# Three in four rows of attention's shift and scale summed by TensorE in four column quarters, on one Trainium2 core

## The chip, the core and the metric

The kernel is one block of a hybrid model (short convolution, sparse attention, adaptive layer norm, gated feed-forward) in float32 on one core of a Trainium2 chip. The metric is the device time of one execution, in microseconds. The engines are TensorE (PE in the profile, with its weight loads as PEld), VectorE (DVE), ScalarE (ACT), GpSimd (POOL) and SyncE (SP), which here only issues loads.

## The reference

```python
def rms_norm(x, g):
    xf = x.astype(jnp.float32)
    y = xf * lax.rsqrt(jnp.mean(xf * xf, axis=-1, keepdims=True) + EPS)
    return (y * g.astype(jnp.float32)).astype(x.dtype)

def modulate(h, shift, scale):
    return h * (1.0 + scale[:, None, :]) + shift[:, None, :]
...
sh_a, sc_a, g_a, sh_f, sc_f, g_f = jnp.split(jax.nn.silu(c) @ ada_w[l] + ada_b[l], 6, axis=-1)
h = modulate(rms_norm(x, norm_mix[l]), sh_a, sc_a)
proj = h @ w_in[l]
...
x = x + g_a[:, None, :] * (jnp.concatenate([y_conv, y_attn], axis=-1) @ w_out[l])
h = modulate(rms_norm(x, norm_ffn[l]), sh_f, sc_f)
x = x + g_f[:, None, :] * ((jax.nn.silu(h @ ffn_w1[l]) * (h @ ffn_w3[l])) @ ffn_w2[l])
```

There are 512 tokens and a model width of 2048; `c` is one vector of 2048, `ada_w` is 2048 x 12288, `w_in` is 2048 x 5656. The change concerns `sh_a` and `sc_a`, that is 2 x 2048 columns of `silu(c) @ ada_w`, 33.5 MB of weights.

## The kernel before, in words

Width 2048 is 16 chunks of 128 (`KC`). The start stage loads the four token tiles of x, gets each token's norm on ScalarE, and turns x into 16 chunks `xnT` (channels on partitions, tokens along the row) by float32 multiplications with a diagonal (L278). Then, two chunks at a time (`STEP`), it needs their shift and scale, modulates them on ScalarE (L293), splits the result into a rounded part and its rest (`ahi` L295, `alo` L296), and multiplies with the columns of w_in for raw keys and values, gate logits, selected keys and the first half of the queries. Every such product is three matmuls of 512 columns in the float32r form (L98 to L100, `mm3`), and the weights are split the same way as they are loaded (`load_split`, L91 to L93).

The shift and scale of two chunks come from `start_steps`: twice (scale, then shift) a sum over 2048 rows of a 256-column piece of ada_w. Partition p holds rows 16p to 16p + 15, so there are 16 rows k to add on each partition (a load of 512 KB brings four), and then a sum over partitions. Of the 16, `SHARE` = 6 are scaled by ScalarE (L183) and added by POOL (L185); the other 10 are multiplied and added by DVE (L187, L189), and L192 joins the two. `ada_cols` turns the sum by TensorE (L206, two 128-column transposes), and DVE adds along the row (L208), adds the bias (L210) and, for the scale, applies the norm's gain (L213).

`weave` (the generator helper) sets the order in which the code is written: after each piece of the projections of two chunks (`start_columns`), so many steps of the sums of the next two. Tile's scheduler then reorders each engine's instructions by its own estimates, so what stands in each engine's queue is not what the loop says. Loads of all kinds go through SP's queue in one order; a load that waits for a buffer holds those behind it. The ring of ada_w has four buffers of 512 KB, that of w_in four. TensorE starts its matmuls in queue order. The eight PSUM banks are four `main` buffers, which hold the raw keys and values over the whole stage, and four `aux` buffers, one of which holds the gate logits.

Of the kernel before, what the change touches and what calls it, by code (L numbers as in the profile page):

```python
# [9 lines left out]
F32 = mybir.dt.float32  # L10
F32R = mybir.dt.float32r
I32 = mybir.dt.int32
AF = mybir.ActivationFunctionType
ALU = mybir.AluOpType
# [3 lines left out]
P = 128  # L18
D = 2048
S = 512  # L20
NT = S // P
KC = D // P
# [47 lines left out]
def block_kernel(ctx: ExitStack, tc: tile.TileContext, a: dict, out: bass.AP):  # L70
    nc = tc.nc
# [4 lines left out]
    def pool(name, bufs=1, stack=ctx, **kw):  # L76
        return stack.enter_context(tc.tile_pool(name=name, bufs=bufs, reuse_waits="tile", **kw))
# [24 lines left out]
    def weave(work, side, n):  # L102

        due = 0.0
        for _ in work:
            due += n
            while due >= 1:
                next(side, None)
                due -= 1
        for _ in side:  # L110
            pass
# [14 lines left out]
    ring = rings(ctx, 4, 3)  # L126
    accp = pool("acc", 2)
# [4 lines left out]
    st0 = ExitStack()  # L132
    sp = pool("start", 1, stack=st0)
    cT = cp.tile([P, KC], F32, name="cT")
# [11 lines left out]
    ident, causal = const[:, 0:P], const[:, P:2 * P]  # L146
# [3 lines left out]
    inv, ones = const[:, o:o + HD // 2], const[:, o + HD // 2:o + HD // 2 + P]  # L150
# [7 lines left out]
    cols = cp.tile([P, nrow], F32, name="cols")  # L158
    bcol = cp.tile([P, NB6], F32, name="bcol")
    gsc = cp.tile([P, 2, KC], F32, name="gsc")  # L160
    shf = cp.tile([P, 2, KC], F32, name="shf")
    gts = cp.tile([P, NT, 3 * NH], F32, name="gts")

    ada_v = ada_w.rearrange("(p k) n -> p k n", k=KC)

    def ada_steps(ring, width, c0, n, bias=False, second=None, share=0):


        acc = accp.tile([P, 512], F32, tag="acc", name="acc")[:, :n]
        acc2 = second.tile([P, 512], F32, tag="acc2", name="acc2", bufs=2)[:, :n] if share else None  # L170
        step = min(width // n, KC)
        yield acc
        if bias:
            nc.gpsimd.memset(acc, 0.0)
            nc.sync.dma_start(acc[0:1, :], a["ada_b"][:, c0:c0 + n])
        for k0 in range(0, KC, step):
            raw = ring.tile([P, width], F32, tag="araw", name="araw")
            rv = raw[:, :step * n].rearrange("p (k n) -> p k n", k=step)
            nc.sync.dma_start(rv, ada_v[:, k0:k0 + step, c0:c0 + n])
            for k in range(k0, k0 + step):  # L180
                w, s = rv[:, k - k0, :], cT[:, k:k + 1]
                if k < share:
                    nc.scalar.activation(w if k else acc2, w, AF.Copy, scale=s)  # L183
                    if k:
                        nc.gpsimd.tensor_add(acc2, acc2, w)  # L185
                elif k == share and not bias:
                    nc.vector.tensor_scalar(acc, w, s, None, op0=ALU.mult)  # L187
                else:
                    nc.vector.scalar_tensor_tensor(acc, w, s, acc, op0=ALU.mult, op1=ALU.add)  # L189
            yield  # L190
        if share:
            nc.vector.tensor_add(acc, acc, acc2)  # L192

    def ada(*args, **kw):
        steps = ada_steps(*args, **kw)
        acc = next(steps)
        for _ in steps:
            pass
        return acc

    def ada_cols(psum_tile, acc, which, m, k0, n):

        ps = psum_tile()
        for c in range(n):
            cs = slice(c * P, (c + 1) * P)
            nc.tensor.transpose(ps[:, cs], acc[:, cs], ident)  # L206
        d = (gsc if m else shf)[:, which, k0:k0 + n]
        nc.vector.reduce_sum(d, ps[:, :n * P].rearrange("p (c q) -> p c q", c=n), axis=AX)  # L208
        b0 = (which * 3 + m) * KC + k0
        nc.vector.tensor_add(d, d, bcol[:, b0:b0 + n])  # L210
        if m:
            g0 = at[("norm_mix", "norm_ffn")[which]] + k0
            nc.vector.scalar_tensor_tensor(d, d, 1.0, cols[:, g0:g0 + n], op0=ALU.add, op1=ALU.mult)  # L213
# [14 lines left out]
    ksv = kp.tile([P, NT, 512], F32, name="ksv")  # L228
    q0 = kp.tile([P, NT, 512], F32, name="q0")
    raw_kv = kp.tile([P, 2, NKV, S], F32, name="raw_kv")  # L230
    aring = pool("araw", 4, stack=st0)
    STEP, AW, SHARE = 2, 1024, 6

    def start_steps(k0):

        if k0 < KC:
            for m in (1, 0):
                steps = ada_steps(aring, AW, m * D + k0 * P, STEP * P, second=sp, share=SHARE)
                acc = next(steps)
                yield from steps  # L240
                ada_cols(aux, acc, 0, m, k0, STEP)

    first = start_steps(0)
    vrow = sp.tile([nrow, P], F32, name="vrow")
    brow = sp.tile([NB6, P], F32, name="brow")
    at, r0 = {}, 0
# [13 lines left out]
    for i in range(NT):  # L260
# [8 lines left out]
        dg = sp.tile([P, P], F32, name=f"dg{i}")  # L269
        nc.vector.tensor_scalar(dg, ident, ss, None, op0=ALU.mult)  # L270
        dgs.append(dg)
    for _ in range(KC * STEP * P // AW):
        next(first)
    xnT = []
    for k in range(KC):
        ps = aux()
# [6 lines left out]
    hT = []  # L283
    ps_kv = [main() for _ in range(4)]
    ps_gl = aux()
    for _ in first:
        pass

    def start_columns(k0):
        n = STEP  # L290
        for k in range(k0, k0 + n):
            h = sp.tile([P, S], F32, tag="h", name="h", bufs=2)
            nc.scalar.activation(h, xnT[k], AF.Identity, scale=gsc[:, 0, k:k + 1], bias=shf[:, 0, k:k + 1])  # L293
            hi, lo = parts()
            nc.scalar.copy(hi, h)  # L295
            nc.vector.tensor_sub(lo, h, hi.bitcast(F32))  # L296
            hT.append((hi, lo))
        w = load_split(ring, rows(w_in, k0, n, CKC, 512), n, 512)
        for c in range(4):
            for kk in range(n):  # L300
                mm3(ps_kv[c], [t[:, kk, c * P:(c + 1) * P] for t in w], hT[k0 + kk], k0 + kk == 0, k0 + kk == KC - 1)
            yield
        w = load_split(ring, rows(w_in, k0, n, CGL, P), n, P)
        for kk in range(n):
            mm3(ps_gl, [t[:, kk, :] for t in w], hT[k0 + kk], k0 + kk == 0, k0 + kk == KC - 1)
        yield

        for c0, dst, ends in ((CKS, ksv, (0, 2, 4, 8, 12, 16)), (CQ, q0, (0, 2, 6, 10, 14, 16))):
            if k0 + n not in ends:
                continue  # L310
            ks = range(ends[ends.index(k0 + n) - 1], k0 + n)
            ws = [load_split(ring, rows(w_in, k, 2, c0, 512), 2, 512) for k in ks[::2]]
            for i in range(NT):
                ps = aux()
                tok = slice(i * P, (i + 1) * P)
                for k in ks:
                    mm3(ps, [h[:, tok] for h in hT[k]], [t[:, k % 2, :] for t in ws[(k - ks[0]) // 2]],
                        k == ks[0], k == ks[-1])
                if k0 == 0:
                    nc.scalar.copy(dst[:, i, :], ps)  # L320
                else:
                    nc.vector.tensor_add(dst[:, i, :], ps, dst[:, i, :])
                yield

    for k0 in range(0, KC, STEP):
        weave(start_columns(k0), start_steps(k0 + STEP), 1.3)
    for m in range(2):
        for g in range(NKV):
            (nc.vector.tensor_copy if g else nc.scalar.copy)(raw_kv[:, m, g, :], ps_kv[m * NKV + g])
# [801 lines left out]
```

## Time and profile before

| | us |
|---|---|
| median of 3 runs | 2312.16 (2307.25 to 2317.63) |
| the profiled execution, its time | 2311.1 |
| its span | 2309.3 |
| TensorE busy in the span | 2234.3 (97%) |
| VectorE | 1681.4 (73%) |
| ScalarE | 960.3 (42%) |
| GpSimd | 132.7 (6%) |

Busy time is an average over stages with different limits, so the whole-span shares say little about the start stage. Matmuls overlap in the records (one of 512 columns lasts about 0.39 us, and the next starts 0.23 us after it), so TensorE's cost is read from the distance between starts or ends, not from busy time. The profile's page names lines of the kernel before; all times of the trace are from the span's start. A few matmul records are missing from the trace.

### The profile page before, as it was taken

The numbers are of one execution on the slowest core, as the hardware profiler recorded it, in microseconds if no ns is written. First come the engines' busy times: TensorE is split into PE (matmuls) and PEld (weight loads), VectorE is DVE, ScalarE is ACT, GpSimd is POOL, SyncE is SP. The second block draws the span as 40 slices with busy tenths as digits, with TensorE's granted clock in tenths as the row PEclk, the third lists the DMA queues.
The fourth block names the chain that finished last, engine by engine and source line by source line (L and its number), as shares of the span: only waits on it lengthen the run. The fifth ranks groups of instructions, "written<-read, shape, count | busy, mean of one in ns | idle before, by whom it ended". The sixth has DMA issues, their size and how long they took to land.

```text
span 2309.3 us, 30022 instructions
## 1 busy us (share of the span) xinstructions
PE 2234.3 (97%) x11225; PEld 1861.8 (81%) x11225; DVE 1681.4 (73%) x2561; ACT 960.3 (42%) x1601; POOL 132.7 (6%) x204
## 2 busy tenths in 40 slices
PE   5889999999999999899999999999999999999999
PEld 4667767778777778788888888888888788888887
DVE  6897738877856783888888888888888655534356
ACT  6544425455444222744444444444444432222221
POOL 2430000000000000000000000000000200000010
PEclk9999999999999999999999999999999999999999
DMA  8884356544533883264334443344442675533243
GB/s 292 262 277 148 98 189 184 165 126 147 147 94 128 301 291 128 87 183 123 119 120 124 123 123 120 119 123 124 123 124 78 216 245 187 182 106 128 92 155 114
DMA packets 374406, 358.60 MB, mean 155 GB/s; under 512 B 14856, under 2 KB 288620, under 8 KB 373236
## 3 DMA queue, kind: packets, MB, share of 16 engines
q1 hardware_dynamic: 365364, 325.22, 44.7%
q0 software_dynamic: 8896, 31.46, 3.9%
q8 instruction: 88, 1.44, 0.2%
q14 instruction: 58, 0.48, 0.1%
HBM read 336.70 MB, written 19.92 MB: 154 GB/s over the span
## 4 chain that ended last, share of the span: by engine, by line
PE 42%; issue 36%; DVE 10%; DMA 9%; ACT 2%; POOL 1%; SPq 0%; DVEq 0%; POOLq 0%; ACTq 0%
PE main L98 8%; PE main L99 8%; PE main L100 8%; DMA araw<-in_ada_w 7%; DVE acc L189 4%; PE aux L98 4%; PE aux L99 4%; PE aux L100 4%; PE aux L646 1%; DVE wlo L93 1%; PE main L834 1%; PE aux L834 1%; PE aux L618 1%; POOL gd L886 1%; DMA raw<-in_w_in 1%
## 5 line engine op out<-in xcount | busy, mean ns | idle before, releaser
L92 ACT CAST whi<-raw 128x1024 fp32r<-128x1024 f32 (+1 forms) x168 | 171.7, 1022 | 486.9 <-PE main L100 265.9
L93 DVE TENSOR_TENSOR wlo<-raw,whi 128x1024 fp32r<-128x1024 f32 (+1 forms) x168 | 200.4, 1193 | 223.2 <-ACT whi L92 221.7
L834 PE MATMUL main<-hC,whi 128*128 128x512 f32 x1408 | 356.2, 395 | 5.5 <-DVE hC L851 3.3
L827 DVE TENSOR_TENSOR wlo<-raw,whi 128x1024 fp32r<-128x1024 f32 x218 | 265.8, 1220 | 107.1 <-ACT whi L822 107.1
L189 DVE SCALAR_TENSOR_TENSOR acc<-araw,cT,acc 128x512 f32<-128x512 f32 (+1 forms) x392 | 270.8, 692 | 90.1 <-DMA araw<-in_ada_w 79.3
L822 ACT CAST whi<-raw 128x1024 fp32r<-128x1024 f32 x218 | 228.1, 1046 | 259.5 <-PE main L834 129.4
L834 PEld LDWEIGHTS main<-hC,whi 128*128 128x128 f32 x1408 | 254.4, 190 | 52.2 <-DVE hC L851 4.4
L834 PE MATMUL aux<-hC,whi 128*128 128x512 f32 x1072 | 269.5, 393 | 0.0
L834 PEld LDWEIGHTS aux<-hC,whi 128*128 128x128 f32 x1072 | 193.6, 190 | 34.8
L836 PEld LDWEIGHTS main<-hC,wlo 128*128 128x128 f32 x1408 | 192.9, 191 | 13.8
L836 PE MATMUL main<-hC,wlo 128*128 128x256 f32 x1408 | 197.0, 283 | 0.0
L98 PE MATMUL main<-alo,whi 128*128 128x512 f32 x448 | 180.9, 404 | 9.9 <-DVE alo L296 9.9
L100 PE MATMUL main<-ahi,whi 128*128 128x512 f32 x448 | 177.2, 396 | 0.0
L99 PE MATMUL main<-ahi,wlo 128*128 128x512 f32 x448 | 177.0, 395 | 0.0
L836 PEld LDWEIGHTS aux<-hC,wlo 128*128 128x128 f32 x1072 | 146.4, 190 | 10.5
L98 PE MATMUL main<-wlo,ahi 128*128 128x512 f32 x384 | 152.3, 397 | 0.5 <-DVE t L773 0.4
L100 PE MATMUL main<-whi,ahi 128*128 128x512 f32 x384 | 150.6, 392 | 0.0
L99 PE MATMUL main<-whi,alo 128*128 128x512 f32 x384 | 150.6, 392 | 0.0
L836 PE MATMUL aux<-hC,wlo 128*128 128x256 f32 x1072 | 149.8, 282 | 0.0
L822 ACT CAST whi<-t 128x1024 fp32r<-128x1024 f32 x84 | 88.2, 1050 | 136.4 <-PE aux L834 70.9
L98 PE MATMUL main<-wlo,ghi 128*128 128x512 f32 x352 | 138.2, 394 | 3.0 <-ACT ghi L1056 2.7
L98 PE MATMUL aux<-wlo,ghi 128*128 128x512 f32 x352 | 137.8, 391 | 0.0
(273 smaller groups left out, 3818.8 us busy)
## 6 DMA issues: line engine op xcount, KB each, us to landing
raw<-in_ffn_w SPq DMA_DIRECT2D x264, 512.0 KB
araw<-in_ada_w SPq DMA_DIRECT2D x136, 512.0 KB
araw<-in_ada_w SPq DMA_DIRECT2D x112, 256.0 KB
raw<-in_w_in SPq DMA_DIRECT2D x128, 192.0 KB
raw<-in_w_in SPq DMA_DIRECT2D x40, 512.0 KB
raw<-in_w_out SPq DMA_DIRECT2D x32, 512.0 KB
gd<-d POOLq DMA_DIRECT2D x44, 256.0 KB, 2.3
graw<-gd POOLq DMA_DIRECT2D x44, 256.0 KB, 4.1
```

Source lines behind the costliest of these rows:

```text
L92: nc.scalar.copy(hi[:, :m], raw[:, :m])
L93: nc.vector.tensor_sub(lo[:, :m], raw[:, :m], hi[:, :m].bitcast(F32))
L98: nc.tensor.matmul(ps, lhs[0], rhs[1], start=first, stop=False)
L99: nc.tensor.matmul(ps, lhs[1], rhs[0], start=False, stop=False)
L100: nc.tensor.matmul(ps, lhs[0], rhs[0], start=False, stop=last)
L189: nc.vector.scalar_tensor_tensor(acc, w, s, acc, op0=ALU.mult, op1=ALU.add)
L618: nc.tensor.matmul(one[b], queries(g, i, h), kT[b][g][:, :L], start=True, stop=True)
L646: nc.tensor.matmul(po[:, b * HD:(b + 1) * HD], s["pT"][b][:, kb * P:(kb + 1) * P], vv[b][:, kb, g * HD:(g + 1) * HD], start=kb == 0, stop= ...
L822: nc.scalar.copy(hi, t)
L827: nc.vector.tensor_sub(lo, t, hi.bitcast(F32))
L834: nc.tensor.matmul(ps, wt[0][:, ks[k]], hC[p][:, k, :], start=first and k == 0, stop=False, skip_group_check=True)
L836: nc.tensor.matmul(ps[:, HS:], wt[1][:, ks[k]], hC[p][:, k, 0:HS], start=False, stop=last and k == HK - 1, skip_group_check=True)
```

## The change

`start_steps` now sums the scale and the shift of two chunks together. A load brings four rows k of one of them (512 KB as before); two loads fill one buffer of the ring, which has three buffers of 1 MB. Of each four rows, DVE takes the first (`SHARE` = 1) with one instruction over all 512 columns. TensorE takes the other three: `crep` holds `silu(c)` repeated over 32 columns, and a multiplication of these 32 weight columns with 128 columns of ada_w writes 32 PSUM partitions; four of them, one in each quarter of the array's columns, cover the scale and shift of both chunks. All rows k add up in one `aux` buffer. Four more such multiplications, with ones, add DVE's sum. ScalarE copies the 128 x 128 result (each quarter's 32 partitions hold the same row), one multiplication with four columns of the identity turns it (L253), and DVE adds the bias and applies the gain. ScalarE's scalings, POOL's adds, the transposes and the reductions of this part go. The first unit's sums now stand behind the turning of x in the code, and `weave` takes 0.6 steps where it took 1.3 (a unit has 5 steps now, where it had 8). `ada`, which serves the other parts of ada_w, keeps its path without the share.

```diff
-    def ada_steps(ring, width, c0, n, bias=False, second=None, share=0):
+    def ada(ring, width, c0, n, bias=False):
...
-                if k < share:
-                    nc.scalar.activation(w if k else acc2, w, AF.Copy, scale=s)
-                    if k:
-                        nc.gpsimd.tensor_add(acc2, acc2, w)
-                elif k == share and not bias:
+                if k == 0 and not bias:
                     nc.vector.tensor_scalar(acc, w, s, None, op0=ALU.mult)
                 else:
                     nc.vector.scalar_tensor_tensor(acc, w, s, acc, op0=ALU.mult, op1=ALU.add)
...
-    aring = pool("araw", 4, stack=st0)
-    STEP, AW, SHARE = 2, 1024, 6
+    aring = pool("araw", 3, stack=st0)
+    STEP, SHARE = 2, 1
+    AK, AN = 4, STEP * P
+    crep = sp.tile([P, KC, 32], F32, name="crep")
+    nc.vector.tensor_copy(crep, cT[:, :, None].to_broadcast([P, KC, 32]))
...
-        if k0 < KC:
-            for m in (1, 0):
-                steps = ada_steps(aring, AW, m * D + k0 * P, STEP * P, second=sp, share=SHARE)
-                acc = next(steps)
-                yield from steps
-                ada_cols(aux, acc, 0, m, k0, STEP)
...
+        ps = aux()
+        acc = accp.tile([P, 512], F32, tag="acc", name="acc")
+        begun = [False] * 4
+
+        def quarter(lhs, src, last):
+            for j in range(4):
+                nc.tensor.matmul(ps[32 * j:32 * j + 32, :P], lhs, src[:, j * P:(j + 1) * P], start=not begun[j], stop=last,
+                                 skip_group_check=True)
+                begun[j] = True
+
+        for k in range(0, KC, AK):
+            raw = aring.tile([P, AK, 2 * AN], F32, tag="araw", name="araw")
+            for m in range(2):
+                c0 = m * D + k0 * P
+                nc.sync.dma_start(raw[:, :, m * AN:(m + 1) * AN], ada_v[:, k:k + AK, c0:c0 + AN])
+            for kk in range(AK):
+                w, s = raw[:, kk, :], cT[:, k + kk:k + kk + 1]
+                if kk >= SHARE:
+                    quarter(crep[:, k + kk, :], w, False)
+                elif k + kk == 0:
+                    nc.vector.tensor_scalar(acc, w, s, None, op0=ALU.mult)
+                else:
+                    nc.vector.scalar_tensor_tensor(acc, w, s, acc, op0=ALU.mult, op1=ALU.add)
+            yield
+        quarter(ones[:, 0:32], acc, True)
+        asb = sp.tile([P, P], F32, tag="asb", name="asb", bufs=2)
+        nc.scalar.copy(asb, ps[:, :P])
+        nc.tensor.matmul(ps[:, AN:AN + 4], asb, ident[:, 0:P:32], start=True, stop=True, skip_group_check=True)
+        yield
+        for m, d in ((1, gsc), (0, shf)):
+            d = d[:, 0, k0:k0 + STEP]
+            nc.vector.tensor_add(d, ps[:, AN + m * STEP:AN + (m + 1) * STEP], bcol[:, m * KC + k0:m * KC + k0 + STEP])
+            if m:
+                g0 = at["norm_mix"] + k0
+                nc.vector.scalar_tensor_tensor(d, d, 1.0, cols[:, g0:g0 + STEP], op0=ALU.add, op1=ALU.mult)
...
-        weave(start_columns(k0), start_steps(k0 + STEP), 1.3)
+        weave(start_columns(k0), start_steps(k0 + STEP), 0.6)
```

Two places show how the instructions move. On TensorE, in the start stage before, between the projections of the first two chunks (`main` and `aux` are the PSUM buffers, the numbers tell buffers apart, L206 are the transposes of a sum):

```order
L100 MATMUL main_312<-ahi_366,whi_371 128x512
L206 MATMUL aux_432<-const_87,acc_382 128x128 x2
L98 MATMUL aux_313<-alo_361,whi_450 128x512
L99 MATMUL aux_313<-ahi_360,wlo_451 128x512
L100 MATMUL aux_313<-ahi_360,whi_450 128x512
```

Two transposes there stand for each 16 rows of a scale or shift.

On TensorE after the change, at the end of the projections of the third and fourth chunk (L232 are the quarters, `acc` is DVE's sum, `asb` the copied result of a unit, L253 the turn):

```order
L100 MATMUL aux_717<-whi_656,ahi_575 128x512
L232 MATMUL aux_597<-acc_598,const_87 32x128 x4
L232 MATMUL aux_765<-araw_767,crep_108 32x128 x12
L232 MATMUL aux_765<-araw_795,crep_108 32x128
L253 MATMUL aux_597<-const_87,asb_729 128x4
L232 MATMUL aux_765<-araw_795,crep_108 32x128 x11
L98 MATMUL aux_835<-wlo_825,ahi_569 128x512
L99 MATMUL aux_835<-whi_824,alo_570 128x512
L100 MATMUL aux_835<-whi_824,ahi_569 128x512
```

A unit's last four quarters and its turn now have quarters of the next unit between and behind them. Over the whole stage TensorE's queue has 416 quarters; 64 stand ahead of the first projection matmul, and the other 352 in 33 runs of 1 to 33, each ended by a matmul of another kind.

On SP, from the first load of ada_w, before:

```order
L179 DMA araw<-in_ada_w 128x4x256 x8
L91 DMA raw<-in_w_in 128x2x512
L179 DMA araw<-in_ada_w 128x4x256 x5
L91 DMA raw<-in_w_in 128x2x128
L179 DMA araw<-in_ada_w 128x4x256
```

and after:

```order
L240 DMA araw<-in_ada_w 128x4x256 x6
L91 DMA raw<-in_w_in 128x2x512
L91 DMA raw<-in_w_in 128x2x128
L91 DMA raw<-in_w_in 128x2x512 x3
L91 DMA raw<-in_w_in 128x2x128
L91 DMA raw<-in_w_in 128x2x512
L240 DMA araw<-in_ada_w 128x4x256 x12
```

Six loads, which fill the three buffers, go first; seven loads of w_in have moved ahead of the next twelve, of which two are the first unit's last.

## Rows read from the trace of the kernel before

**Rows 1.** Busy time by stretch: us, engines busy (count), granted clock, DMA share, GB/s.

```profile
core 0: us, PE busy (x) PEld busy (x) DVE busy (x) ACT busy (x) POOL busy (x), PEclk, DMA share, GB/s
20.00:30.00 10.00, 10.00 (x85) 10.00 (x85) 8.26 (x15) 7.79 (x17) 5.21 (x8) 1.00 0.77 247
...
43.30:185.70 142.40, 123.40 (x506) 96.45 (x506) 133.32 (x238) 74.05 (x136) 57.56 (x68) 0.94 0.81 271
170.00:180.00 10.00, 10.00 (x45) 8.09 (x44) 9.86 (x19) 6.22 (x12) 4.18 (x6) 1.00 0.94 332
```

**Rows 2.** The start stage's waits: who for whom, us, times, longest.

```profile
ACT h L293 <- DVE shf L210: 34.6, 8, 7.8
```

**Rows 3.** TensorE's groups by shape in 43.3 to 185.7 us: count, busy, mean ns.

```profile
L98 PE MATMUL aux<-wlo,ahi 128*128 128x512 f32 x90 | 37.6, 418 | 5.0 <-DVE wlo L93 5.0
...
L98 PE MATMUL main<-alo,whi 128*128 128x512 f32 x56 | 23.5, 419 | 9.9 <-DVE alo L296 9.9
...
L98 PE MATMUL aux<-alo,whi 128*128 128x512 f32 x14 | 6.5, 463 | 0.0
...
L206 PE MATMUL aux<-const,acc 128*128 128x128 f32 x26 | 5.2, 281 | 9.1 <-DVE acc L192 9.0
```

**Rows 4.** TensorE's timeline around the partial transposes at L334: start, length.

```profile
218.55 0.39 PE L100 MATMUL aux<-whi,ahi 128*128 128x512 f32 x1
218.87 0.37 PE L334 MATMUL aux<-const,gl 32*128 32x32 f32 x3
219.17 0.50 PE L98 MATMUL main<-wlo,ahi 128*128 128x512 f32 x1
...
219.97 0.39 PE L98 MATMUL main<-wlo,ahi 128*128 128x512 f32 x1
220.29 0.24 PE L334 MATMUL aux<-const,gl 32*128 32x32 f32 x1
220.47 0.50 PE L99 MATMUL main<-whi,alo 128*128 128x512 f32 x1
...
221.04 0.39 PE L98 MATMUL main<-wlo,ahi 128*128 128x512 f32 x1
...
222.41 0.39 PE L98 MATMUL main<-wlo,ahi 128*128 128x512 f32 x1
```

**Rows 5.** TensorE's timeline around ordinary transposes, then one transpose's durations (min/median/max).

```profile
51.22 0.39 PE L100 MATMUL main<-ahi,whi 128*128 128x512 f32 x1
51.45 0.38 PE L206 MATMUL aux<-const,acc 128*128 128x128 f32 x2
51.58 0.48 PE L98 MATMUL aux<-alo,whi 128*128 128x512 f32 x1
...
L206 PE MATMUL aux<-const,acc x64: 270/273/302, 33.9 to 849.1; 128*128 128x128 f32 x64
```

**Rows 6.** DVE's multiply-adds by shape: the start stage's, then those of the whole span.

```profile
L189 DVE SCALAR_TENSOR_TENSOR acc<-araw,cT,acc 128x256 f32<-128x256 f32 x144 | 84.9, 592 | 3.4 <-DMA araw<-in_ada_w 0.9
...
L189 DVE SCALAR_TENSOR_TENSOR acc<-araw,cT,acc 128x512 f32<-128x512 f32 x248 | 185.8, 750 | 86.7 <-DMA araw<-in_ada_w 78.4 <-DMA acc<-in_ada_b 2.5 <-POOL acc L174 2.3
```

**Rows 7.** TensorE's timeline of two float32 groups, then one L572 pass's durations.

```profile
18.54 15.51 PE L278 MATMUL aux<-dg,xt 128*128 128x128 f32 x122 [0.92 <-DVE dg L270]
...
364.55 0.98 PE L572 MATMUL aux<-kcT,qT 128*128 128x32 f32 x8
...
L572 PE MATMUL aux<-kcT,qT x64: 190/276/276, 364.5 to 623.4; 128*128 128x32 f32 x64
```

**Rows 8.** All engines' timeline from the first unit's shift to its first projection matmul.

```profile
39.33 0.15 DVE L210 TENSOR_TENSOR shf<-shf,bcol 128x2 f32<-128x2 f32 x1
...
39.51 1.52 ACT L293 ACTIVATE h<-xnT,shf,gsc 128x512 f32<-128x512 f32 x2 [1.00 <-DVE shf L210]
...
40.94 1.12 ACT L295 CAST ahi<-h 128x512 fp32r<-128x512 f32 x2
...
43.31 0.79 PE L98 MATMUL main<-alo,whi 128*128 128x512 f32 x1 [6.75 <-DVE alo L296]
```

More of the change, by code (lines that the diff above doesn't have):

```diff
@@ L164, in block_kernel @@
     ada_v = ada_w.rearrange("(p k) n -> p k n", k=KC)
-    def ada_steps(ring, width, c0, n, bias=False, second=None, share=0):
+    def ada(ring, width, c0, n, bias=False):
         acc = accp.tile([P, 512], F32, tag="acc", name="acc")[:, :n]
-        acc2 = second.tile([P, 512], F32, tag="acc2", name="acc2", bufs=2)[:, :n] if share else None
         step = min(width // n, KC)
-        yield acc
         if bias:
@@ L189, in ada_steps @@
                     nc.vector.scalar_tensor_tensor(acc, w, s, acc, op0=ALU.mult, op1=ALU.add)
[L190 to L195, printed above, removed]
-        acc = next(steps)
-        for _ in steps:
-            pass
         return acc
@@ L230, in block_kernel @@
     raw_kv = kp.tile([P, 2, NKV, S], F32, name="raw_kv")
-    aring = pool("araw", 4, stack=st0)
-    STEP, AW, SHARE = 2, 1024, 6
-    def start_steps(k0):
-        if k0 < KC:
-            for m in (1, 0):
-                steps = ada_steps(aring, AW, m * D + k0 * P, STEP * P, second=sp, share=SHARE)
-                acc = next(steps)
-                yield from steps
-                ada_cols(aux, acc, 0, m, k0, STEP)
-    first = start_steps(0)
+    aring = pool("araw", 3, stack=st0)
+    STEP, SHARE = 2, 1
@@ new lines, in block_kernel @@
+    AK, AN = 4, STEP * P
+    crep = sp.tile([P, KC, 32], F32, name="crep")
+    nc.vector.tensor_copy(crep, cT[:, :, None].to_broadcast([P, KC, 32]))
+    def start_steps(k0):
+        if k0 >= KC:
+            return
+        ps = aux()
[31 more added lines that the diff above has]
+                nc.vector.scalar_tensor_tensor(d, d, 1.0, cols[:, g0:g0 + STEP], op0=ALU.add, op1=ALU.mult)
@@ L271, in block_kernel @@
         dgs.append(dg)
-    for _ in range(KC * STEP * P // AW):
-        next(first)
     xnT = []
@@ L285, in block_kernel @@
     ps_gl = aux()
-    for _ in first:
+    for _ in start_steps(0):
         pass
```

## The prediction

> **What bounds the kernel now.** I read the span by stretches first, then the start stage alone by engine and by group, then its waits, and last the timelines that price a single matmul. Times are made against the profiled execution, 2311.1 us; the median of the runs, 2312.2 us, is 1.1 us above it. A difference under 0.5% (11.6 us) cannot be told from none here.
>
> From 185.7 us on TensorE issues without gaps; the change leaves that work alone. What it touches lies before. In 43.3 to 185.7 us, from the first projection matmul to the point where gaps end, DVE is busy 133.3 of 142.4 us and DMA 0.81 of the time, 271 GB/s [rows 1]. DVE is the bound: ScalarE waits 34.6 us in 8 pieces for the last vector instruction of a shift before it can modulate a chunk [rows 2].
>
> TensorE has slack there, but not much. The stretch holds 506 matmuls, 480 of them the 512-column ones (160 each at L98, L99, L100) and 26 transposes [rows 1, 3]. Issued without gaps, the 512-column ones come 0.228 us apart (six steps in 1.37 us) [rows 4]. Two transposes of 128 columns span 0.38 us of which one lasts 0.273, so they come 0.107 us apart [rows 5]. So TensorE needs 480 x 0.228 + 26 x 0.107 = 112.2 us, and **30.2 us of the 142.4 are idle or slow**. That is all the change can win while TensorE keeps its work; every microsecond it adds to TensorE comes off it, and beyond it makes the kernel longer.
>
> **What is removed.** DVE loses the 144 multiply-adds of 256 columns at 592 ns, 85 us [rows 6], with their first products, merges and reductions, and gets 64 of 512 columns; such ones last 750 ns elsewhere, 48 us [rows 6]. ScalarE's 96 scalings and POOL's 80 adds go. I cost all this at nothing: it frees engines that are no longer the bound once TensorE has the rows. If TensorE is not the bound, DVE's remainder (133 - 85 + 48, so at most 96 us of 142) is no bound either; DMA would be. The loads of ada_w are the same 64 of 512 KB. DMA reached 332 GB/s in one 10 us stretch [rows 1], so at 271 it has a fifth to spare. On SP the six loads that fit the new ring stand ahead of seven w_in loads, and the last two of the first unit come behind them, once TensorE has read a buffer.
>
> **What is added.** 416 quarter matmuls: 8 units of two chunks, 12 rows in 16 by four quarters, and four more to sum DVE's rows. 64 stand ahead of the first projection matmul, so **352 stand in the stretch**, in 33 runs between other matmuls, by the order above.
>
> One quarter: a float32 multiplication is recorded as two passes with a weight load each: the 64 that turn x are 128 records, 122 of them in 15.51 us; in the 10 us after 20 us 85 run, 0.118 us each [rows 1, 7]. A pass of 128 columns streams no faster than the transposes' 0.107 us. So a quarter is two passes, and four prices are possible. If quarters don't overlap: 2 x 0.118 = 0.236 us. If all four do: 2 x 0.107 / 4 = 0.054. But the two passes of a quarter stand one behind the other in the same columns, and TensorE starts matmuls in order: the second must wait for the first to stream, and only then can the next quarter's first start beside it. That gives one quarter per pass, 0.107. I take **0.11 us**: 352 x 0.11 = 38.7 us.
>
> One run: a quarter uses part of the array, and the trace has one such case, the transposes at L334 that use 32 of its rows. Ends of the 512-column matmuls around three of them are 0.73 us apart (218.55 + 0.39 to 219.17 + 0.50), around a single one 0.61 (219.97 + 0.39 to 220.47 + 0.50) [rows 4]. Less the usual 0.228 that is 0.50 and 0.38: 0.06 for each small transpose and **0.32 us for going into the partial array and back**. Ordinary transposes cost no such thing: 51.22 + 0.39 to 51.58 + 0.48 is 0.45, just 0.228 and two times 0.107 [rows 5]. 33 runs x 0.32 = 10.6 us. Its bounds are 0 (columns are not rows) and 0.4.
>
> The seven turning multiplications (L253) are two passes with full weights; such a pass of few columns comes every 0.10 us ((0.98 - 0.276) / 7) [rows 7]: 7 x 0.2 = 1.5 us. The 26 transposes that go give back 2.8 us.
>
> The first unit: x is turned at TensorE's pace both times, until about 34 us. Then 52 quarters now stand there (5.7 us), the turn (0.2) and a copy on ScalarE before it (0.5, an estimate: a cast of 512 columns takes 0.56 there [rows 8]), and from the shift on the same chain as today, 39.33 to 43.31 us, 4.0 us [rows 8]: the first projection matmul comes at about 44.6, **1.3 us later**. From below: 1.6 us sooner, if its quarters overlap fully (52 x 0.054 = 2.8); from above 8 later, if they don't at all (52 x 0.236 = 12.3).
>
> What stays of the idle 30.2 us: the wait for shift and scale goes, since behind L253 other quarters and matmuls are queued for longer than the 4.0 us chain, and TensorE no longer pauses until its clock falls (0.94 granted over the stretch [rows 1]). New waits come: quarters wait for their load at the head of TensorE's queue with projections behind them, and a unit's accumulator holds one of the four aux buffers for its whole length. I leave 5 us, between 0 and 15, half of today's.
>
> **Sum:** 38.7 + 10.6 + 1.5 - 2.8 + 1.3 - (30.2 - 5) = +24.1 us. From 2311.1 that is 2335; on the median, 2336. The parts' own bounds (0.107 to 0.13 a quarter, 0.15 to 0.4 a run, 0 to 12 us idle) give 2325 to 2353 for this case.
>
> **Rivals.**
>
> - *All four quarters overlap*: 352 x 0.054 = 19.0 in place of 38.7, and the start 1.6 us sooner instead of 1.3 later: +1.5 us, 2314, not slower. For it: nothing in the rows forbids four column groups to stream at once. Against: passes in pairs, in order. "TensorE: Matmul & The Clock Gate" of the Trainium skill (Part 3, measured speedup against the span model) says that packed matmuls overlap, a group taking one matmul's time and about 4 ns for each further tile. No run here shows that yet; by it a group of four would be about 0.226 us, 0.057 a quarter, an estimate, and the sum +3 us.
> - *The same, and going in and out of the quarters is free*: 19.0 + 1.5 - 2.8 - 1.6 - 30.2, with no idle left, = -14.1, 2298, faster. Here DVE's former bound was worth all it looked like. It decides from where 352 quarters and 33 runs together take less than 30.2 - 1.5 + 2.8 + 1.6 = 33 us, and tells from no change below 22; the one row on partial arrays asks 10.6 for the runs alone.
> - *Quarters don't overlap*, so that the change doesn't do what it says: 352 x 0.236 = 83.1 us, and the start 7 us later still: +75 us, 2387. For it: every float32 row of this trace is serial. Against: different columns of the array have no work in common.
> - *TensorE waits for loads*: the order holds runs of up to 33 quarters, nearly the whole ring of three buffers, with projections queued behind. With all 15 us of idle kept, 2346; a loss only if DMA, not TensorE, sets the pace, which its 0.81 speaks against.
>
> **How the numbers follow.** The forecast has 0.50, full overlap 0.22, overlap with free switching 0.09, no overlap 0.13, late loads 0.06. Slower: the forecast but for a tail of 0.05, no overlap, late loads, 0.64. Same: full overlap and that tail, 0.27. Faster: 0.09. The range takes the forecast's own with full overlap below it and late loads above: 2306 to 2360; it leaves out the two ends.
>
> **What would show it.** Right: TensorE without gaps from 45 us on, DVE and POOL well below it; four quarters (eight passes) starting over about 0.44 us; about 0.3 us lost at each entry and exit; the start stage's last projection later by some 24 us, and everything after it shifted by as much. Wrong: eight passes in 0.25 us, or in 0.9; waits of L232 for araw of over 15 us; DVE still above 0.9; or a difference that comes from after the stage.

## The result and the profile after

The changed kernel takes 2328.62 us (median of 4 runs, 2327.02 to 2329.11); the kernel before, run beside it, 2313.31 (4 runs, 2307.25 to 2317.63). The ratio is **1.0067 [1.0043, 1.0091]**: slower by 15.3 us. The forecast was 2336 with a range of 2306 to 2360. The profiled execution took 2329.1 us, its span 2327.2.

The busy time by stretch of the changed kernel (columns as in [rows 1]):

```profile
core 0: us, PE busy (x) PEld busy (x) DVE busy (x) ACT busy (x) POOL busy (x), PEclk, DMA share, GB/s
20.00:30.00 10.00, 10.00 (x71) 10.00 (x71) 3.19 (x5) 3.66 (x7) 0.00 (x0) 1.00 0.96 350
30.00:40.00 10.00, 7.54 (x121) 7.15 (x120) 3.99 (x5) 4.83 (x8) 0.00 (x0) 1.00 0.58 179
40.00:50.00 10.00, 5.31 (x60) 3.82 (x61) 3.18 (x8) 2.81 (x5) 0.00 (x0) 0.59 1.06 369
43.30:185.70 142.40, 138.19 (x1169) 104.78 (x1162) 64.54 (x104) 41.20 (x62) 0.00 (x0) 0.97 0.79 261
```

Against [rows 1], DVE went from 133.3 to 64.5 us of the stage's 142.4 and POOL from 57.6 to nothing. TensorE went from 123.4 to 138.2. The bound moved from DVE to TensorE, as intended, and the kernel got slower all the same. The place where the stage ends shows that the loss is made there. The first of the partial transposes, at 218.87 us in [rows 4], now starts at 233.5 us, **14.6 us later**. By line (durations min/median/max, first and last start):

```profile
L350 PE MATMUL aux<-const,gl x4: 221/232/244, 233.5 to 234.9; 32*128 32x32 f32 x4
```

Most of the 15.3 us between the medians is lost by then. The two traced spans differ by 17.9 us (2327.2 and 2309.3), so 3.3 of these lie behind that point, where both kernels have the same code. ScalarE's wait for the shift, 34.6 us in [rows 2], is mostly gone, and TensorE has a new wait for loads of ada_w (the waits: who for whom, us, times, longest):

```profile
ACT h L309 <- DVE gsc L260: 10.3, 7, 1.9
...
PEld aux L232 <- DMA araw<-in_ada_w: 5.5, 2, 4.2
```

That wait stands at the start. TensorE's timeline there (start, length, idle before and its releaser), against [rows 8]:

```profile
35.37 2.17 PE L232 MATMUL aux<-araw,crep 128*32 128x128 f32 x72
41.49 0.44 PE L232 MATMUL aux<-araw,crep 128*32 128x128 f32 x4 [3.95 <-DMA araw<-in_ada_w]
42.92 1.28 PE L232 MATMUL aux<-araw,crep 128*32 128x128 f32 x18 [0.98 <-DMA araw<-in_ada_w]
...
45.20 0.59 PE L253 MATMUL aux<-const,asb 128*128 128x4 f32 x2 [0.36 <-ACT asb L252]
...
49.09 0.79 PE L98 MATMUL main<-alo,whi 128*128 128x512 f32 x1 [1.85 <-DVE alo L312]
```

The first projection matmul comes at 49.09, not 43.31: 5.8 us later. DMA fills the three buffers at 350 GB/s until 30 us and falls to 179 in the next 10, for the first unit's quarters stand behind all turning of x in TensorE's queue, and no buffer is free before they have run. The last two loads of the unit start only then, and TensorE stands 3.95 and 0.98 us for them.

The rest arises between the projections. Of the timeline, a run of 12 quarters (24 passes), one of four and one of a single quarter, each between two 512-column matmuls:

```profile
55.78 0.39 PE L100 MATMUL main<-ahi,whi 128*128 128x512 f32 x1
56.10 0.86 PE L232 MATMUL aux<-araw,crep 128*32 128x128 f32 x24
56.90 0.50 PE L98 MATMUL aux<-alo,whi 128*128 128x512 f32 x1
...
65.66 0.39 PE L100 MATMUL aux<-whi,ahi 128*128 128x512 f32 x1
65.98 0.42 PE L232 MATMUL aux<-acc,const 128*32 128x128 f32 x8
66.33 0.50 PE L98 MATMUL aux<-wlo,ahi 128*128 128x512 f32 x1
...
118.83 0.39 PE L100 MATMUL aux<-whi,ahi 128*128 128x512 f32 x1
119.15 0.41 PE L232 MATMUL aux<-araw,crep 128*32 128x128 f32 x2
119.49 0.50 PE L98 MATMUL main<-alo,whi 128*128 128x512 f32 x1
```

From end to end (start plus length) the 512-column matmuls around them are 1.23, 0.78 and 0.77 us apart. Less the usual 0.228, a run of 12 quarters costs 0.99 us (more exactly than these rounded rows), one of four 0.557, one of one **0.54**. Four quarters cost hardly more than one: the four column groups stream at once. Two passes that follow each other in the same columns are 0.107 apart, so four quarters in the four groups cost 2 x 0.107 = 0.214, and what stays of 0.54 is 0.32 for going in and out. Longer runs of other kernels below fit this: 24 quarters 1.65, 28 quarters 1.86. The law is

**run = 0.32 + 0.214 for each started group of four + some 0.01 per group.**

I summed what lies between the ends of following 512-column matmuls beyond 0.228, from the first projection to the 550th: 32.9 us before, 41.3 after, so 8.4 more. With the 5.8 of the start that is 14.2 of the 14.6. The 41.3 are: 38.2 in the runs and turns, 2.4 in 12 matmuls at half clock (0.2 too long each; the granted clock is 0.59 in 40 to 50 us), 0.7 elsewhere. By the law, the 33 runs with their 99 started groups and the turns make 21.2 + 10.6 + 1.5 = 33.3 of the 38.2; the other 4.9 are waits, of turns for their copy and of quarters for loads.

### The profile page after: what moved, and what is told of

Read it like the earlier page. It is cut to its first block, busy times and chain, and to the rows that moved or that the text cites. A ratio compares the mean times of both kernels' runs of the same rounds, so it can differ in the third digit from the quotient of the medians.

```text
span 2327.2 us, 31192 instructions
## 1 busy us (share of the span) xinstructions
PE 2267.6 (97%) x12041; PEld 1883.5 (81%) x12041; DVE 1601.8 (69%) x2402; ACT 923.5 (40%) x1513; POOL 64.6 (3%) x124
## 4 chain that ended last, share of the span: by engine, by line
PE 48%; issue 35%; DMA 8%; DVE 6%; ACT 2%; POOL 1%; SPq 0%; POOLq 0%; DVEq 0%; ACTq 0%
PE main L98 8%; PE main L99 8%; PE main L100 8%; DMA araw<-in_ada_w 6%; PE aux L98 5%; PE aux L99 4%; PE aux L100 4%; DVE acc L182 2%; PE aux L662 1%; POOL gd L902 1%; PE aux L634 1%; PE aux L232 1%; PE aux L850 1%; PE main L850 1%; DMA graw<-gd 1%
## 5 line engine op out<-in xcount | busy, mean ns | idle before, releaser
L182 DVE SCALAR_TENSOR_TENSOR acc<-araw,cT,acc 128x512 f32<-128x512 f32 x248 | 185.8, 750 | 84.9 <-DMA araw<-in_ada_w 76.9
L852 PEld LDWEIGHTS main<-hC,wlo 128*128 128x128 f32 x1408 | 192.6, 191 | 13.9
```

The source lines that it names most:

```text
L852: nc.tensor.matmul(ps[:, HS:], wt[1][:, ks[k]], hC[p][:, k, 0:HS], start=False, stop=last and k == HK - 1, skip_group_check=True)
```

## The experiments

None leaves out work. In each expectation "Theory A" is the author's own account, and "rival" the one set against it. Ratios are to the kernel before, run on the same chip as the experiment; its median was 2312.2 us beside e1 to e4, 2313.7 beside e5 to e10 and 2315.9 beside e11 and e12, so compare kernels of different sets by their ratios. "Stage ends" is the start of the first partial transpose in each kernel's one trace (218.9 before).

| kernel | us | ratio | stage ends, us |
|---|---|---|---|
| changed kernel | 2328.62 | 1.0067 [1.0043, 1.0091] | 233.5 |
| e1_first_early | 2317.89 | 1.0026 [1.0015, 1.0037] | 227.2 |
| e2_by_quarter | 2340.70 | 1.0123 [1.0105, 1.0142] | 245.8 |
| e3_share2 | 2322.80 | 1.0053 [1.0039, 1.0066] | 229.5 |
| e4_fewer_runs | 2352.22 | 1.0174 [1.016, 1.0188] | 259.5 |
| e5_share2_early | 2314.45 | 0.9997 [0.9985, 1.0009] | 219.3 |
| e6_turn_sooner | 2317.45 | 1.0016 [1.0006, 1.0026] | 223.7 |
| e7_no_te_rows | 2304.82 | 0.9955 [0.994, 0.9971] | 210.1 |
| e8_few_early | 2310.14 | 0.9987 [0.9978, 0.9996] | 216.9 |
| e9_few_early_share2 | 2316.82 | 1.0008 [0.9998, 1.0018] | 223.1 |
| e10_few_early_share3 | 2333.59 | 1.0085 [1.0071, 1.0099] | 238.2 |
| e11_tail_less | 2309.28 | 0.9963 [0.9949, 0.9977] | 213.1 |
| e12_tail_least | **2302.08** | **0.994 [0.9926, 0.9953]** | 206.2 |

From the end of the stage to the end of the span the 14 traces take between 2088.5 us (e1) and 2095.6 (e11), with 2090.4 before and 2093.7 after the change, although the kernels differ in the start stage alone. So times of single executions differ by some us behind the stage; why is not shown, and gains of the stage are read from the last column.

### Does the order of the quarters matter?

e2 writes the same quarters of a step by column group instead of by row, so that the passes of one group of columns stand together:

```diff
-                    quarter(crep[:, k + kk, :], w, False)
+                    continue
...
+            for j in range(4):
+                for kk in range(SHARE, AK):
+                    nc.tensor.matmul(ps[32 * j:32 * j + 32, :P], crep[:, k + kk, :], raw[:, kk, j * P:(j + 1) * P], ...)
```

> The changed kernel with the same 416 quarters, but written column group by column group: the three rows of a step for the first quarter of the columns, then the three for the second, and so on. Theory A (a quarter costs 0.049 us because the four column groups stream at once, each pass taking about 0.107 us in its own columns): 12 quarters then take some 2.2 us in place of 0.6, 352/12 x 1.6 = +47 us, about 2375 us. Rival (a pass with 32 weight columns is short by itself, 0.025 us, in whichever columns it stands): the time stays within 5 us of 2328.6. In between, by the passes per run in the trace.

Measured: 2340.70 us, 12 more than the changed kernel, between the two expectations. Runs of 12, 6 and 3 quarters in its timeline of TensorE:

```profile
56.86 0.39 PE L100 MATMUL main<-ahi,whi 128*128 128x512 f32 x1
57.17 1.59 PE L251 MATMUL aux<-araw,crep 128*32 128x128 f32 x24
58.69 0.50 PE L98 MATMUL aux<-alo,whi 128*128 128x512 f32 x1
...
99.46 0.39 PE L100 MATMUL aux<-whi,ahi 128*128 128x512 f32 x1
99.78 1.09 PE L251 MATMUL aux<-araw,crep 128*32 128x128 f32 x12
100.80 0.50 PE L98 MATMUL aux<-wlo,ahi 128*128 128x512 f32 x1
...
110.11 0.39 PE L100 MATMUL aux<-whi,ahi 128*128 128x512 f32 x1
110.43 0.84 PE L251 MATMUL aux<-araw,crep 128*32 128x128 f32 x6
111.20 0.50 PE L98 MATMUL aux<-wlo,ahi 128*128 128x512 f32 x1
```

Read as above, six passes in the same columns cost 0.97, which is 0.54 and four times 0.107. Six more in the next columns add only 0.25, where a queue strictly in line would add 0.64; 24 passes cost 1.72, where the order by row takes 0.99. In the trace the first pass in the next columns starts with the third of the six, before their last three. So, if the queue holds them as they are written (the scheduler may reorder, and the queue's order was not read here), TensorE lets passes wait for their columns while later ones start in others, but not without limit; "in queue order" is then too strong for passes in different columns. What sets the 0.25 stays open.

### Is the start the other part?

e1 issues the first unit's steps between the turns of x, so that buffers come free early:

```diff
     xnT = []
+    first = start_steps(0)
     for k in range(KC):
...
+        if k % 4 == 3:
+            next(first)
...
-    for _ in start_steps(0):
+    for _ in first:
         pass
```

> The changed kernel, but the first unit's four load steps are written between the turning of x (one after every fourth chunk) instead of behind it; nothing is left out. Theory A (the start is 5.8 us later because the ring of three buffers is held until TensorE has turned all of x, so the first unit's last loads come late): the first projection matmul moves from 49.1 us to 43 to 45 us and the time from 2328.6 to about 2323.5 us. Rival (the start is late because 52 quarters and the longer chain stand in the way, whatever the loads): the first projection matmul stays within 1.5 us of 49.1, and the time within 2 us.

```profile
24.38 0.86 PE L232 MATMUL aux<-araw,crep 128*32 128x128 f32 x24
...
38.06 0.86 PE L232 MATMUL aux<-araw,crep 128*32 128x128 f32 x24
...
43.21 0.50 PE L98 MATMUL main<-alo,whi 128*128 128x512 f32 x1 [2.07 <-DVE alo L315]
```

In its timeline of TensorE no quarter waits for the first loads any more, and the first projection is at 43.21 us, where Theory A put it. The time fell by 10.7 us, more than the 5 to 6 that the start holds. At the end of the stage 6.3 us of the trace are won. The rest lies behind the stage, where the changed kernel's trace takes 2093.7 us and e1's 2088.5, the shortest of all; nothing shows that the edit caused this.

e3 gives DVE a second row in four (`STEP, SHARE = 2, 2`), which takes 128 of the 416 quarters away; e5 has both edits.

> The changed kernel with two of four rows on VectorE instead of one (288 quarters in all, not 416); nothing is left out. Theory A (TensorE sets the pace of the start stage, a quarter costs it 0.049 us and a run 0.44): some 110 quarters and 4 runs fewer behind the first projection matmul, -5.4 - 1.8, about 2321 us; VectorE goes from 43% to some 60% busy there. Rival (VectorE's sums set when shift and scale are ready): 32 more products of 512 columns at 0.75 us, 24 us, show in the time, 2335 us or more.

> The first unit's steps between the turning of x and two rows in four on VectorE, both at once; nothing is left out. Theory (the two gains lie in different places, the start and TensorE's time in the stage, so they add): the early start gave 10.7 us and the second row 5.8 us, so 2328.6 - 16.5 = about 2312 us, level with the kernel before. Rival (one bound lies behind both, so that the second gains nothing once the first is there): 2318 us.

e3 is 5.8 us faster than the changed kernel, e5 14.2 (2314.45), 3.4 better than e1. The gains add, nearly; at the end of the stage e1 and e3 win 6.3 and 4.0 us, and e5 14.2. With both the kernel is where it was before.

### Is it the number of runs?

e4 collects the quarters of two steps in one run and gives a unit two runs:

```diff
                 if kk >= SHARE:
-                    quarter(crep[:, k + kk, :], w, False)
+                    late.append((crep[:, k + kk, :], w))
...
+            if k + AK == KC:
+                late.append((ones[:, 0:32], acc))
+            if k // AK % 2:
+                with behind():
+                    for lhs, w in late:
+                        quarter(lhs, w, lhs is late[-1][0] and k + AK == KC)
+                late.clear()
...
-        weave(start_columns(k0), start_steps(k0 + STEP), 0.6)
+        weave(start_columns(k0), start_steps(k0 + STEP), 0.36)
```

(`behind()` keeps TensorE's matmuls, those of the projections too, in the written order, and the turn is now written one step behind the copy.)

> The changed kernel with the same 416 quarters in fewer runs: two steps' quarters together, VectorE's sum with the second, and TensorE's order held to the written one, so that 14 runs stand behind the first projection matmul instead of 33, and 18 to 36 other matmuls between a unit's copy and its turn. Theory A (each run costs 0.44 us for going into the column groups and back, and the turn waits for the copy some 3 us in all): 19 x 0.44 + 3, about -11 us, 2318 us. Rival (a run costs next to nothing by itself, what is lost around it are waits for loads): no gain, and longer waits, since two of the three buffers are held until both are read: 2328 us or more.

It missed, widely: 2352.22 us. TensorE's timeline at a unit's turn, and the wait that grew (from the waits after 50 us):

```profile
116.94 0.39 PE L100 MATMUL aux<-whi,ahi 128*128 128x512 f32 x1
117.16 0.28 PE L268 MATMUL aux<-const,asb 128*128 128x4 f32 x2
122.42 0.80 PE L98 MATMUL main<-alo,whi 128*128 128x512 f32 x1 [4.98 <-DVE alo L326]
```

```profile
PE main L98 <- DVE alo L326: 26.6, 6, 5.0
```

In this order the turn (L268) is the last matmul before the projections that need its result. The chain of shift, modulation and splitting, 4.0 us in [rows 8], stands bare, six times, and the half clock behind it (granted 0.60 from 122.4 to 126.0 us, after TensorE stood 4.98) makes 54 matmuls slow (0.43 apart, 0.2 too long each, 10.7 us in all). The cover for which the prediction let this wait go, matmuls queued behind the turn, is needed: here is its price. e6 changes the places alone: the steps are issued behind pieces 0, 3 and 4 of the projections, so that projections follow the turn.

> The kernel with few runs, but each unit's steps placed after the first, fourth and fifth piece of the projections, so that 54 other matmuls stand behind its turn and not none. Theory A (the few runs did save 0.32 us each, and what cost 24 us there was the chain from the turn to the next projection, about 5.3 us in six units, with the clock falling to its lower level and 54 matmuls at 0.43 us): both go, some 35 to 40 us off 2352, 2313 to 2320 us. Rival (the pairs hold the ring too long and the loads come late): 2335 us or more, with waits of the quarters for araw in place of the chain.

```profile
113.11 0.39 PE L100 MATMUL main<-ahi,whi 128*128 128x512 f32 x1
113.43 1.52 PE L238 MATMUL aux<-araw,crep 128*32 128x128 f32 x48
114.88 0.50 PE L98 MATMUL main<-alo,whi 128*128 128x512 f32 x1
...
122.15 0.39 PE L100 MATMUL aux<-ahi,whi 128*128 128x512 f32 x1
122.38 0.28 PE L268 MATMUL aux<-const,asb 128*128 128x4 f32 x2
122.52 0.47 PE L98 MATMUL aux<-wlo,ahi 128*128 128x512 f32 x1
```

2317.45 us, 35 below e4 and 11.2 below the changed kernel. 24 quarters in one run cost 1.65 us, where two runs of 12 take 2 x 0.99, and behind the turn the next matmul starts at once. e8 adds e1's early start (steps behind the 8th and 12th turn of x):

> Few runs with the turn placed sooner, and the first unit's steps between the turning of x; three rows in four on TensorE as in the change, nothing left out. Theory A (the change's loss lies in its start and in its runs and chains, not in the quarters themselves): 2317.5 less 6 to 10 us, 2308 to 2312 us, no slower than the kernel before. Rival (TensorE's quarters cost more than the idle time holds): 2315 us or more.

Measured 2310.14, ratio 0.9987 [0.9978, 0.9996], with TensorE busy for 140.7 of the stage's 142.4 us. **The change as it is, three rows in four on TensorE, loses nothing once its two faults are mended**, and wins nothing worth naming: what DVE gave back is spent on quarters.

### Where do the rows belong?

e7 takes no rows of the data to TensorE: DVE keeps them, with ScalarE and POOL for six of 16 as before, but in this kernel's pieces of 512 columns, with the early start and one step after each piece of the projections; TensorE only sums the two accumulators by quarters.

```diff
-                if kk >= SHARE:
-                    quarter(crep[:, k + kk, :], w, False)
+                if kk == 3 or kk == 2 and k // AK % 2 == 0:
+                    nc.scalar.activation(w if k + kk > 2 else acc2, w, AF.Copy, scale=s)
+                    if k + kk > 2:
+                        nc.gpsimd.tensor_add(acc2, acc2, w)
...
-        quarter(ones[:, 0:32], acc, True)
+        quarter(ones[:, 0:32], acc, False)
+        quarter(ones[:, 0:32], acc2, True)
```

> The changed kernel's merged sums (scale and shift in one instruction of 512 columns, summed over partitions by quarters with ones, first unit early, a step after each piece), but no row of ada_w on TensorE: ten of 16 on VectorE, six on ScalarE and GpSimd as before the change; nothing is left out. Theory A (what the change brings to VectorE comes from the merging as much as from the rows, and every run on TensorE costs): 7 runs of 8 quarters, 7 x (0.32 + 0.43), 1.5 for the turns and up to 5 of waits for copies in place of 30 us of idle: 2293 to 2302 us, faster than both. Rival (the sums of ten rows on VectorE still set the pace): 2308 to 2318 us, with VectorE at 0.9 or more in the stage.

2304.82 us, 0.9955 [0.994, 0.9971]: faster than both kernels, but short of what was expected. Its group of multiply-adds (count, busy, mean ns) says why, and two stretches:

```profile
L249 DVE SCALAR_TENSOR_TENSOR acc<-araw,cT,acc 128x512 f32<-128x512 f32 x72 | 80.7, 1121 | 3.8 <-DMA araw<-in_ada_w 2.2
```

```profile
100.00:120.00 20.00, 18.65 (x96) 14.69 (x95) 19.69 (x24) 9.93 (x15) 7.42 (x5) 1.00 0.76 261
120.00:140.00 20.00, 19.59 (x101) 15.47 (x100) 18.68 (x24) 10.70 (x17) 7.45 (x5) 1.00 0.93 318
```

The multiply-add that takes 750 ns elsewhere takes 1121 on average here, and DVE is nearly full again in these stretches (122.7 of 142.4 us in the stage). That GpSimd's adds are the cause shows within this trace: three multiply-adds beside them take 4.58 us, and the next two, after the adds have ended at 109.00, take 1.52.

```profile
102.79 6.21 POOL L245 TENSOR_TENSOR acc<-acc,araw 128x512 f32<-128x512 f32 x4 [9.76 <-ACT araw L243]
104.97 4.58 DVE L249 SCALAR_TENSOR_TENSOR acc<-araw,cT,acc 128x512 f32<-128x512 f32 x3
110.08 1.52 DVE L249 SCALAR_TENSOR_TENSOR acc<-araw,cT,acc 128x512 f32<-128x512 f32 x2
```

Of the 72, the 27 that overlap no GpSimd instruction average 747 ns, and the 43 that overlap some for half of their time or more 1373. The kernel before shows the same: of its 144 multiply-adds of 256 columns (592 ns on average, [rows 6]), 91 overlap none and average 482, and 49 overlap some for half or more and average 807. So the rows that POOL took there were not free: they cost DVE some 144 x 0.11 = 16 us, an estimate.

e9 and e10 are e8 with two and three rows in four on DVE (`SHARE` 2 and 3), and no POOL:

> The same with two rows in four on VectorE. Theory A (TensorE sets the pace, four quarters cost 0.21 us): per unit four groups of four less, 7 x 0.86 = -6 us against the one before it, about 2303 us. Rival (loads of ada_w set the pace by now): no gain, with waits of L238 for araw.

> The same with three rows in four on VectorE, one on TensorE. Theory A: another 6 us, about 2297 us. Rival (12 rows of 512 columns at 0.75 us, 9 us a unit, beside VectorE's 8 to 9 us of other work bring back VectorE as the bound): as the one before it or slower, with TensorE waiting for acc at the last quarters of a unit.

Theory A missed twice: 2316.82 and 2333.59, worse with every row that leaves TensorE; for e10 the rival had it right, with the wait that it named. The lists of what the quarters' line waits for give that wait (us, times), first e9, then e10:

```profile
  DVE acc L254: 18.1, 14
```

```profile
  DVE acc L254: 45.5, 14
```

```profile
145.57 1.06 PE L238 MATMUL aux<-araw,crep 128*32 128x128 f32 x16
149.64 0.65 PE L238 MATMUL aux<-acc,const 128*32 128x128 f32 x8 [3.02 <-DVE acc L254]
```

These lists count a wait twice, for the weight load and for its matmul. The matmuls alone wait 8.1 us in e9 and 21.8 in e10 for the accumulator, about what the stage ends later than in e8 (6.2 and 21.3); so the "18 us" of e11's expectation is about twice the wait. For loads, e9's rival, they wait 2.1 us in e8, 3.3 in e9 and 0.6 in e10. In e10's timeline the last quarters, which sum DVE's accumulator, stand at the head of TensorE's queue while DVE still multiplies the rows of the unit's last loads. So e11 and e12 give DVE the rows of early loads, not of late ones, and put those last quarters one piece of the projections later:

```diff
-    STEP, SHARE = 2, 1
+    STEP, SHARE = 2, (4, 3, 2, 1)
...
-                if kk >= SHARE:
+                if kk >= SHARE[k // AK]:
```

(the form of e12; e11 has 3, 2, 2, 1)

> Few runs and an early start, with VectorE's eight rows of 16 taken mostly from the first loads of a unit (three, two, two, one) and its sum brought in by four quarters one piece later. Theory (what the even halves lost was TensorE standing at the last quarters until VectorE had added four rows behind the last load, 18 us in the trace): those waits go, and the price by runs and groups of four is 0.32 + 0.64, 0.32 + 1.07, 0.53 and a turn of 0.22 a unit, 22 us in the stage in place of 29: about 2303 us. Rival (the waits are for loads, whoever adds them): 2310 us or more, with waits of L238 for araw.

> The same with ten rows on VectorE (four, three, two, one). Theory: one group of four less twice a unit, 18 us in the stage: about 2300 us. Rival (VectorE, 10 x 0.75 us a unit more beside some 8 us of other work, falls behind): slower than the one before it, with waits for acc again.

e11: the matmuls' wait for the accumulator is down to 0.2 us, and the stage ends 10.0 us sooner than in e9. The time, 2309.28 us, is six more than expected: against e8, from which the expectation counts, the stage ends 3.8 us sooner and not 7, and the part behind the stage was the longest of all traces. e12: **2302.08 us**, nearly as expected (its stage ends 10.7 us sooner than in e8, where 11 were expected), 0.994 [0.9926, 0.9953], faster than the kernel before by 13.9 us. In e12 the wait for the accumulator does not show at all. Which of the two edits removed it, the rows' place or the later quarters, no run separates. The multiply-adds of e12, and its stage:

```profile
L254 DVE SCALAR_TENSOR_TENSOR acc<-araw,cT,acc 128x512 f32<-128x512 f32 x72 | 53.9, 749 | 2.9 <-DMA araw<-in_ada_w 1.5
```

```profile
43.30:185.70 142.40, 141.49 (x937) 108.77 (x936) 98.47 (x153) 49.19 (x73) 1.08 (x3) 1.00 0.82 278
```

The 72 multiply-adds are as many as in e7, at 749 ns without GpSimd beside them: 27 us of DVE less. TensorE is busy for all but 0.9 us of the stretch at full clock, and what its matmuls lose beyond 0.228 came down from 41.3 us in the changed kernel to 22.2.

## Why the prediction was right, and where it was wrong

**Direction, place and bound: right.** TensorE became the bound, DVE fell to 45% of the stage and POOL to nothing, the wait for shift and scale mostly went, and 14.6 of the 17.9 us between the two traces arise before the partial transposes. The price of going in and out of the quarters, 0.32 us, read from transposes that use 32 of the array's rows, holds for 32 of its columns to the digit: 33 runs, 10.6 us. "TensorEngine Tiling (Array Packing)" of the Trainium skill (Tiling Modes, Key Properties) says that a change of the tiling mode drains the engine, without a figure; the runs agree in that each visit costs, and give the size. That a drain is what costs it, no run shows.

**The price of a quarter: wrong by half.** The step that failed is "the second must wait for the first to stream, and only then can the next quarter's first start beside it. That gives one quarter per pass, 0.107." The first half is so: six passes in the same columns are (0.97 - 0.54) / 4 = 0.107 apart in e2. The second is not: the next quarters start although the earlier one's second pass still waits, and eight passes take 0.557 us where two take 0.54. All eight start within 0.15 us (0.42 from the first start to the last end in the row above, less the 0.27 of one pass). The prediction named 0.44 us as a sign of being right and 0.25 as one of being wrong, and by that sign it was wrong. A quarter in a full group of four costs 0.054, the price of the first rival. Counted run by run, the 33 runs hold 99 started groups (88 full ones would do; runs that cut a group add the rest): 99 x 0.214 = 21.2 us, not 38.7. "TensorE: Matmul & The Clock Gate" of the Trainium skill (Part 3, measured speedup against the span model) gives about 4 ns for each further tile. Measured are 17 ns for three further quarters of two passes, some 6 each: the rule that the prediction set against its own step was the better one.

**The start: wrong by 4.5 us.** The prediction saw that "the last two of the first unit come behind them, once TensorE has read a buffer", and priced only the 52 quarters left. It did not follow when that is: after all of x has been turned. The first projection came 5.8 us later, not 1.3 (its own terms add up to some 1.1); e1 shows the cause by taking it away.

**What stays of the idle time: 8.0 us, not 5**, inside the bounds of 0 to 15: 4.9 of waits inside the runs, 2.4 of half clock behind the late start, 0.7 elsewhere. A slip did no harm: "at most 96 us" for DVE takes off all 144 multiply-adds, of which the stretch holds 120; 64.5 were measured.

The sum with the measured terms is 21.2 + 10.6 + 1.5 - 2.8 + 5.8 - (30.2 - 8.0) = +14.1 us; the trace has +14.6, the medians +15.3. The forecast of +24 was too high because a term 17.5 us too dear met two that were 4.5 and 3.0 too cheap. That it came out inside its range is in part luck: the errors offset each other.

**The rivals.** The first, full overlap, had the mechanism right and the time (2314) wrong: it had the start 1.6 us sooner where it came 5.8 later, 5 us of idle where 8.0 stayed, and only full groups, 19.0 us, where cut ones make 21.2. Free switching fell with the 0.54 us of a single quarter, serial quarters with the 0.557 of four. Late loads are real, but at the start and not in the stage; TensorE stood 4.9 us for them there, not 15.

## What to carry to other kernels

Quarters are cheap in fours and dear in small runs: with the column groups taken in turn four cost 0.21 us, but each visit between full matmuls costs 0.32 more, so collect them in few runs, put other matmuls behind the turn that ends a unit (bare, its chain costs 5 us a time), and read load buffers early enough for the next loads to start. An engine freed of work is worth only what the wait for it was: share rows so that TensorE and VectorE both end a unit on time (in e12 VectorE has ten rows in 16, most of them of early loads), and look at what an "idle" helper costs its neighbour before it is counted as free.

## What the hardware showed that was not expected

- Column groups overlap fully with float32 passes in order of rows, and in part (0.25 us for six further passes instead of 0.64) even where the passes of one group stand together; what limits that is open.
- VectorE's multiply-add of 512 columns took 1121 ns on average in e7, where GpSimd adds, and 749 in e12, where it doesn't (72 of them each); within e7 it took 747 alone and 1373 beside GpSimd's work for half of its time or more. "GPSIMD Engine Reference" of the Trainium skill (Specifications) says that GpSimd shares its SBUF interfaces with VectorE and contends with vector instructions that have two SBUF inputs, as this one has; the runs agree and give a size. In the kernel before, 256 columns took 482 ns alone and 807 beside such adds.
